# The first layer's feed-forward stage also splits the second mixer's weights, which then come ready split from DRAM

## The chip, the cores and the metric

The kernel runs on one core of a Trainium2 chip. The metric is the device time of one execution in microseconds (us), the median of three runs. All weights and the input lie in DRAM (HBM) when the execution starts, already rearranged on the host.

## The reference

Two blocks follow each other on x, 512 tokens by 1024 channels, in float32. The first has two layers, each a mixer and a feed-forward stage; the second has two layers with other mixers, cross attention and a gated feed-forward stage. The change touches layers 0 and 1 of the first block:

```python
for l in range(2):
    h = rmsnorm(x, norm_mix_g[l])
    proj = h @ w_in[l]                              # 1024 x 4896
    (qa, ka, va, qd, kd, vd, beta_logit, decay_logit, z, gate_logit) = split(proj)
    y_attn = grid_attention(rope(rms(qa)), rope(rms(ka)), va) @ w_o_attn[l]
    qd, kd, vd = silu(conv5(concat(qd, kd, vd)))    # depthwise over tokens
    qd, kd = l2norm(qd), l2norm(kd)
    o = bidir_gated_deltanet(qd, kd, vd, beta, g)   # chunks of 64 tokens, both directions
    y_dn = (rmsnorm(o) * silu(z)) @ w_o_dn[l]
    x = x + (gates[0] * y_attn + gates[1] * y_dn) @ w_out[l]
    h = rmsnorm(x, norm_ffn_g[l])
    u_gate, u_val = split(conv3(h @ w_up[l]))       # 1024 x 5632
    x = x + (silu(u_gate) * u_val) @ w_down[l]      # 2816 x 1024
```

## The kernel before, in words

x is kept transposed, as eight tiles of 128 channels by 512 tokens. Each float32 factor of a large product is split in two parts, a rounded one (hi, type float32r) and the rest (lo), and a product is three matmuls: hi by hi, hi by lo, lo by hi. Activations are split once a stage; weights are split as they are used.

The weights lie in groups of 256 output columns: a group of 1024 input rows is 1 MB, on 128 partitions. `wload` (L464) takes one group. `fetch` (L459, the DMA at L461, on SyncE's queue, SP) brings it into a raw tile `wraw`, of which there are two. Then it is cut into four pieces of 128x512 (four k-chunks of 128 rows by 128 output columns): a copy on ScalarE (ACT, L474) rounds a piece to `whi`, and a subtraction on GpSimd (POOL, the helper `tt`, L383) leaves the rest in `wlo`. There are four buffers of each. `proj` (L480) then issues 12 matmuls for each piece (L487, L490, L491), so that a group is 48 matmuls for two output tiles. Products go to PSUM tiles `psb`, `psf` and `ps`.

The stages come one after the other: m0 (mixer, layer 0), f0 (feed-forward, layer 0), m1, f1, and then the second block. In the profiled execution f0 runs from about 500 to 900 us and m1 from about 900 to 1400.

The feed-forward stage is `ffn`. `up_pair` makes two of 22 middle tiles out of two weight groups: convolution of three taps on ACT and DVE (L588, L589), a gate, a split of the product into `mid`. `down` calls `out_proj` for the products back into x, four groups at a time. The order in the program is five calls of `up_pair`, `down(0)`, four `up_pair`, `down(1)`, two `up_pair`, `down(2)`: 34 groups.

The mixer is `_mix`. Its 19 groups of `win` are, by number: 0 to 3 the query and key tiles of the delta net (`qk_pair`), 4 and 5 its values (`vproj`), 6 and 7 attention's queries, 8 its keys and values, 9 and 10 the output gate z, 11 to 18 the two branch gates (`gate_logits`). `conv_tile` (L697) has a convolution of five taps on DVE; `l2` norms queries and keys; `inside` makes each chunk's inner products and their decays, with tiles `s3`, `gr`, `kt` and `nt` (L843 and after), and stores them to DRAM scratch tiles dnscr (L850, L851), scrK (L836), scrN (L855) and scrT (L863), all on SP; `solve` loads N from scrN and scrT and inverts 64x64 triangles on DVE. `rs_cols` and `rsqrt` make reciprocal roots by integer arithmetic and Newton steps on small 128x16 tiles on DVE (`rc`, `rsq`; L394, L397, L398 and the helper L383). In `_mix`, generators that yield a number are interleaved by a small scheduler that balances those numbers.

The final order of each engine's instructions and of the SP queue is set by the tile framework's scheduler with its own simulated timeline: it may pull an instruction ahead of others as far as buffers allow. On the chip each engine, and each DMA queue, works in its order.

Of the kernel before, what the change touches and what calls it, by code (L numbers as in the profile page):

```python
# [11 lines left out]
F32 = mybir.dt.float32  # L12
# [8 lines left out]
P = 128  # L21
# [23 lines left out]
def _pack_cols(w, kc, cg):  # L45

    w = np.asarray(w)
    L, K, N = w.shape
    g = N // cg
    a = w.reshape(L, kc, P, g, cg).transpose(0, 3, 2, 1, 4)  # L50
    return np.ascontiguousarray(a).reshape(L, g, P, kc * cg)


# [152 lines left out]
def host_arrays(inputs):  # L206
    g = lambda k: np.asarray(inputs[k])
    A = {}
    A["x"] = np.ascontiguousarray(g("x")[0].T).reshape(8, P, S)
    A["mem"] = _pack_cols(np.asarray(g("mem_2")).transpose(0, 2, 1), 8, NMEM)[0, 0]  # L210
    A["vec"] = _vec_layout(inputs)[1]
    A["cst"] = CST_ARR
    A["rope"] = np.ascontiguousarray(_rope_tables())
    A["rett"] = _ret_tables()
    A["hgm"] = _hg_masks()
    A["dsat"] = _dsa_tables()
    A["relb"] = np.concatenate([g("rel_bias_2"), np.ones((1, 8), np.float32)], axis=0)
# [12 lines left out]
    A["wod"] = _pack_cols(by_head(g("w_o_dn").transpose(0, 2, 1)).transpose(0, 2, 1), 4, 128)  # L230
    A["wout"] = _pack_cols(g("w_out"), 8, 256)
    A["wup"] = _pack_cols(g("w_up"), 8, 256)
    for nm, key in (("wdn", "w_down"), ("fdn", "ffn_w_out_2")):
        w = g(key)
        A[nm] = np.concatenate([_pack_cols(w[:, :1024], 8, 256), _pack_cols(w[:, 1024:2048], 8, 256)], axis=1)
        A[nm + "c"] = _pack_cols(w[:, 2048:], 6, 256)
# [3 lines left out]
    A["evin"] = _pack_cols(np.concatenate(ev, axis=2).reshape(1, D, 4096), 8, 256)  # L240
    A["evout"] = _pack_cols(np.concatenate([eo[:, 1 - i, h] for i, h in EV_HEADS], axis=1), 8, 256)

    od = g("od_w_in_2").reshape(1, D, 3, 8, P).transpose(0, 1, 3, 2, 4).reshape(1, D, 3072)
    A["odin"] = _pack_cols(od, 8, 256)
    A["odout"] = _pack_cols(g("od_w_out_2"), 8, 256)
    A["xaq"] = _pack_cols(g("xa_w_q_2"), 8, 256)
    A["xakv"] = _pack_cols(g("xa_w_kv_2"), 8, 256)
    A["xao"] = _pack_cols(g("xa_w_o_2"), 8, 256)
    A["fup"] = _pack_cols(g("ffn_w_in_2"), 8, 256)
    return A  # L250
# [55 lines left out]
class Prog:  # L306
    def __init__(self, ctx, tc, A, out, first):
# [10 lines left out]
        self.dr = pool("dr", 1, space=DRAM)  # L318
        self.ph = None

        self.vect = self.cp.tile([P, NVEC], F32, name="vect")
# [136 lines left out]

    def fetch(self, src, kc, cg):  # L459
        raw = self.wr.tile([P, kc, cg], F32, name="wraw", tag="wraw")  # L460
        self.nc.sync.dma_start(out=raw, in_=src.rearrange("p (k c) -> p k c", k=kc))  # L461
        return raw

    def wload(self, src, kc, cg, rows=False):  # L464


        nc = self.nc
        raw = self.first.pop(0) if self.first else self.fetch(src, kc, cg)
        step, width = (2, cg) if rows else (4, min(P, cg))

        def piece(k, o):
            part = raw[:, k:min(k + step, kc), o:o + width]
            hi, lo = (self.whl.tile(list(part.shape), F32R, name=n, tag=n) for n in ("whi", "wlo"))
            nc.scalar.copy(hi, part)  # L474
            self.tt(lo, part, hi.bitcast(F32), ALU.subtract, "gpsimd")
            return k, hi, lo

        return [[piece(k, o) for k in range(0, kc, step)] for o in range(0, cg, width)]

# [50 lines left out]
    def out_proj(self, wsrc, acts, nxt, k0=0, scale=None, final=True, behind=None):  # L530
        nc = self.nc
        kc = len(acts)
        for g in range(4):
            ws = self.wload(wsrc[g][:, k0 * 256:(k0 + kc) * 256], kc, 256)
# [23 lines left out]
    def ffn(self, l, second, nm, nxt):  # L558
# [3 lines left out]
        with self.phase("ffn") as fp, self.banks(2, 2):  # L562
# [48 lines left out]
            def up_pair(mp):  # L611
                wg = self.wload(wup[mp], 8, 256)
                wv = self.wload(wup[11 + mp], 8, 256)
                for j in range(2):
                    v = (up2 if second else up1)(2 * mp + j, wg[j], wv[j])
                    mid = self.gs("mid", 12, (P, 2, S), F32R)
                    self.split(mid, v)
                    mids[2 * mp + j] = mid

            def down(gi):  # L620
# [12 lines left out]
            for mp in range(9, 11):  # L633
                up_pair(mp)
            down(2)

# [5 lines left out]
    def _mix(self, l, nm, nxt, mp):  # L642
        nc, tc = self.nc, self.tc
        win = self.A["win"][l]
        col = lambda name, n=64: mp.tile([P, n], F32, name=name)
        blk64 = self.c("blk64")
# [55 lines left out]
        def qk_pair(g, first, a):  # L702
            ws = self.wload(win[g], 8, 256)
            for j in range(2):
# [100 lines left out]
        def vproj():  # L805
            for g in range(4, 6):
                ws = self.wload(win[g], 8, 256)
                for j in range(2):
# [80 lines left out]
        def qkv():  # L889


            ws = self.wload(win[8], 8, 256)
            kr, sq = gained(ws[0], f"kg{l}")
# [17 lines left out]
        def queries(g):  # L911


            ws = self.wload(win[6 + g], 8, 256)
            qs = []
# [66 lines left out]
        def zproj():  # L982
            for g in range(9, 11):
                ws = self.wload(win[g], 8, 256)
                for j in range(2):
# [9 lines left out]
        def gate_logits(base, res, make):  # L995
            for g in range(4):
                ws = self.wload(win[base + g], 8, 256)
                for j in range(2):
# [621 lines left out]
    def _cross(self, l, nm, nxt, xp):  # L1620
# [51 lines left out]
        for h in range(4):  # L1672
# [14 lines left out]
            ws = self.wload(wkv[4 + h], 8, 256, rows=True)  # L1687
            vt = [gs("vt", 4, (P, 2, M), F32R) for _ in range(2)]
            pv = [self.psb() for _ in range(2)]
            for t in range(2):  # L1690
                tok = slice(t * P, (t + 1) * P)
                o = pv[t][:, :M]
                for k, hi, lo in ws[0]:
                    for i in range(2):
# [95 lines left out]
```

## Time and profile before

| | |
|---|---|
| median of three runs | 3457.84 us (3456.24 to 3459.11) |
| profiled execution | 3445.89 us |
| its span | 3444.1 us |
| TensorE (PE) busy | 3227.7 us, 94% |
| VectorE (DVE) busy | 2030.8 us, 59% |
| ScalarE (ACT) busy | 1483.2 us, 43% |
| GpSimd (POOL) busy | 1806.1 us, 52% |
| DMA | 342.53 MB, mean 99 GB/s |

The span is the time from the first to the last instruction of the profiled execution. Busy times are of the whole span; the share of one stage can be far from them, so that a stage is read from a cut of the span into stretches. POOL's largest group in the page is the subtraction wlo<-wraw,whi, 1044 instructions and 1369.1 us, and ACT's largest is the cast whi<-wraw, 1044 instructions and 631.5 us.

### The profile page before, as it was taken

How to read it: one execution, taken by the hardware profiler on the slowest of the kernel's cores; microseconds unless marked ns; L12 is line 12 of the kernel's file. 1: busy time of each engine (PE TensorE's matmuls, PEld its weight loads, DVE VectorE, ACT ScalarE, POOL GpSimd, SP SyncE). 2: the span in 40 equal slices, each digit the busy share in tenths (PEclk: the TensorE clock that was granted, in tenths of full speed). 3: DMA queues.
4: the chain of work that ended last, by engine and by line, in shares of the span. 5: the costliest groups of instructions: out<-in, count | busy, mean ns of one | idle time of the engine just before them, and what ended most of it. 6: DMA issues, size and time to landing. Idle time of an engine off the chain costs nothing. (4 is left out here: it accounts for less than half of the span.)

```text
span 3444.1 us, 46891 instructions
## 1 busy us (share of the span) xinstructions
PE 3227.7 (94%) x17342; PEld 2655.6 (77%) x17342; DVE 2030.8 (59%) x3571; ACT 1483.2 (43%) x2766; POOL 1806.1 (52%) x1493
## 2 busy tenths in 40 slices
PE   8888899999987889999999898999999998999999
PEld 6666778888766667788877776878888887888887
DVE  8988555554698866464466676553223786653222
ACT  4526534343553553443353325443334444544332
POOL 4653365444565434654456556565556335555554
PEclk9999999999998999999999998999999999999999
DMA  4532542222354234222232113223223212222222
GB/s 148 160 89 62 119 127 98 98 89 92 121 158 124 73 81 133 100 99 92 98 112 86 62 47 103 85 99 121 94 98 107 78 67 101 88 87 98 98 97 87
DMA packets 135869, 342.53 MB, mean 99 GB/s; under 512 B 43056, under 2 KB 80304, under 8 KB 106969
## 3 DMA queue, kind: packets, MB, share of 16 engines
q1 hardware_dynamic: 134208, 336.04, 30.5%
q10 hardware_dynamic: 1432, 3.49, 0.4%
q8 instruction: 138, 2.26, 0.3%
q14 instruction: 91, 0.74, 0.1%
HBM read 312.15 MB, written 29.97 MB: 99 GB/s over the span
## 5 line engine op out<-in xcount | busy, mean ns | idle before, releaser
L383 POOL TENSOR_TENSOR wlo<-wraw,whi 128x512 fp32r<-128x512 f32 (+2 forms) x1044 | 1369.1, 1316 | 1397.9 <-ACT whi L474 1359.6
L474 ACT CAST whi<-wraw 128x512 fp32r<-128x512 f32 (+2 forms) x1044 | 631.5, 608 | 1129.5 <-PE psb L490 835.2
L487 PE MATMUL psb<-act,whi 128*128 128x512 f32 x1888 | 758.8, 402 | 59.6 <-DVE x L383 19.6
L491 PE MATMUL psb<-act,wlo 128*128 128x512 f32 x1888 | 751.5, 399 | 3.2 <-POOL wlo L383 3.0
L490 PE MATMUL psb<-act,whi 128*128 128x512 f32 x1888 | 752.6, 399 | 0.8 <-DVE act L277 0.6
L487 PEld LDWEIGHTS psb<-act,whi 128*128 128x128 f32 x1888 | 363.5, 193 | 140.0 <-issue 43.4
L491 PEld LDWEIGHTS psb<-act,wlo 128*128 128x128 f32 x1888 | 362.2, 192 | 81.1 <-POOL wlo L383 5.6
L490 PEld LDWEIGHTS psb<-act,whi 128*128 128x128 f32 x1888 | 363.4, 192 | 75.0 <-DVE act L277 2.3
L383 DVE TENSOR_TENSOR x<-psb,x 128x512 f32<-128x512 f32 x168 | 115.2, 689 | 377.0 <-PE psb L491 376.6
L487 PE MATMUL ps<-act,whi 128*128 128x512 f32 (+1 forms) x720 | 280.7, 390 | 3.4 <-ACT rB L303 3.4
L491 PE MATMUL ps<-act,wlo 128*128 128x512 f32 (+1 forms) x720 | 280.2, 389 | 0.0
L490 PE MATMUL ps<-act,whi 128*128 128x512 f32 (+1 forms) x720 | 280.2, 389 | 0.0
L487 PE MATMUL psb<-mid,whi 128*128 128x512 f32 x704 | 276.7, 394 | 1.0 <-DVE x L383 1.0
L491 PE MATMUL psb<-mid,wlo 128*128 128x512 f32 x704 | 276.2, 392 | 0.0
L490 PE MATMUL psb<-mid,whi 128*128 128x512 f32 x704 | 273.6, 389 | 0.0
L487 PEld LDWEIGHTS ps<-act,whi 128*128 128x128 f32 (+1 forms) x720 | 133.9, 186 | 33.7 <-ACT rB L303 4.6
L491 PEld LDWEIGHTS ps<-act,wlo 128*128 128x128 f32 (+1 forms) x720 | 133.9, 186 | 29.4
L490 PEld LDWEIGHTS ps<-act,whi 128*128 128x128 f32 (+1 forms) x720 | 133.9, 186 | 29.1
L491 PEld LDWEIGHTS psb<-mid,wlo 128*128 128x128 f32 x704 | 132.1, 188 | 30.5
L487 PEld LDWEIGHTS psb<-mid,whi 128*128 128x128 f32 x704 | 132.3, 188 | 29.3 <-DVE x L383 1.5
L490 PEld LDWEIGHTS psb<-mid,whi 128*128 128x128 f32 x704 | 132.1, 188 | 29.5
L383 DVE TENSOR_TENSOR cv<-ps,cv 128x512 f32<-128x512 f32 (+1 forms) x60 | 41.5, 692 | 175.9 <-PE ps L491 106.5
(437 smaller groups left out, 5712.3 us busy)
## 6 DMA issues: line engine op xcount, KB each, us to landing
wraw<-in_wup SPq DMA_DIRECT2D x44, 1024.0 KB, 4.8
wraw<-in_fup SPq DMA_DIRECT2D x44, 1024.0 KB, 4.8
wraw<-in_win SPq DMA_DIRECT2D x38, 1024.0 KB, 5.0
wraw<-in_wdn SPq DMA_DIRECT2D x16, 1024.0 KB, 4.8
wraw<-in_evin SPq DMA_DIRECT2D x16, 1024.0 KB, 4.8
wraw<-in_xakv SPq DMA_DIRECT2D x16, 1024.0 KB, 4.9
wraw<-in_fdn SPq DMA_DIRECT2D x16, 1024.0 KB, 4.8
wraw<-in_odin SPq DMA_DIRECT2D x12, 1024.0 KB, 4.9
```

The lines of the kernel that those rows point to most:

```text
L383: getattr(self.nc, eng).tensor_tensor(out, a, b, op)
L474: nc.scalar.copy(hi, part)
L487: mm = nc.tensor.matmul(ps, hi[:, i], acts[k][:, 0, :n], start=k == 0, stop=False)
L490: nc.tensor.matmul(ps, hi[:, i], acts[k][:, 1, :n], start=False, stop=False)
L491: nc.tensor.matmul(ps, lo[:, i], acts[k][:, 0, :n], start=False, stop=k == kc - 1)
```

## The change

Three things are changed.

The host lays weight groups out so that each piece of four k-chunks by 128 columns lies together on a partition (`_pack_tiles`); `fetch` then makes `wraw` of shape (128, columns/128, k-chunks, 128), and `out_proj` passes the k-range that it wants instead of a slice. The splitting of a piece is moved to a helper `parts`, and the cross attention's value groups, which take pieces of two k-chunks by 256 columns, to a helper `wrows`.

`split_ahead` is a generator made in `ffn` of layer 0. For each of the 19 groups of `win` of layer 1 it makes a DRAM tile of two halves; for each half it loads 512 KB into `araw` (three buffers), rounds it on ACT into the first part of a tile `ahl` (two buffers), subtracts on POOL into its second part, and stores both parts, 1 MB, to DRAM. One group is taken after each `up_pair` and after each group of `out_proj`, through `self.side`, 19 calls in all before `down(2)`.

In layer 1, `wgroup` calls `wload_split`: each piece's hi and lo come by a DMA of 256 KB each (128x512) from that DRAM tile directly into `whi` and `wlo`. ACT and POOL do nothing for them.

By the program's counts POOL issues 1460 instructions instead of 1498, ACT 2608 instead of 2646, SP 831 instead of 622; PE and DVE have the same numbers.

The core of the diff:

```diff
+def _pack_tiles(w, kc):
+
+    a = _pack_cols(w, kc, 256)
+    L, g = a.shape[:2]
+    return np.ascontiguousarray(a.reshape(L, g, P, kc, 2, P).transpose(0, 1, 2, 4, 3, 5)).reshape(L, g, P, kc * 256)
...
-    A["win"] = _pack_cols(np.concatenate([kd, qd, vd, qa, ka, va, z, gate], axis=-1), 8, 256)
+    A["win"] = _pack_tiles(np.concatenate([kd, qd, vd, qa, ka, va, z, gate], axis=-1), 8)
...
+    def fetch(self, src, kc, cg, k0=0, n=None):
+
+        n, w = n or kc, min(P, cg)
+        raw = self.wr.tile([P, cg // w, n, w], F32, name="wraw", tag="wraw")
+        self.nc.sync.dma_start(out=raw, in_=src.rearrange("p (j k c) -> p j k c", k=kc, c=w)[:, :, k0:k0 + n])
+        return raw
+
+    def parts(self, part):
+
+        nc = self.nc
+        hi, lo = (self.whl.tile(list(part.shape), F32R, name=n, tag=n) for n in ("whi", "wlo"))
+        nc.scalar.copy(hi, part)
+        self.tt(lo, part, hi.bitcast(F32), ALU.subtract, "gpsimd")
+        return hi, lo
+
+    def split_ahead(self, pool, name, groups):
+
+        nc = self.nc
+        for i, src in enumerate(groups):
+            dst = self.dr.tile([P, 2, 2, 1024], F32, name=f"{name}{i}")
+            self.ahead[name, i] = dst
+            for j in range(2):
+                raw = pool.tile([P, 1024], F32, name="araw", tag="araw", bufs=3)
+                nc.sync.dma_start(out=raw, in_=src[:, j * 1024:j * 1024 + 1024])
+                t = pool.tile([P, 2, 1024], F32R, name="ahl", tag="ahl", bufs=2)
+                nc.scalar.copy(t[:, 0], raw)
+                self.tt(t[:, 1], raw, t[:, 0].bitcast(F32), ALU.subtract, "gpsimd")
+                nc.sync.dma_start(out=dst[:, j], in_=t.bitcast(F32))
+            yield
+
+    def wload_split(self, src):
+
+        def piece(j, k):
+            hi, lo = (self.whl.tile([P, 4, P], F32R, name=n, tag=n) for n in ("whi", "wlo"))
+            for i, t in enumerate((hi, lo)):
+                self.nc.sync.dma_start(out=t.bitcast(F32), in_=src[:, j, i, k * P:(k + 4) * P].rearrange("p (k c) -> p k c", c=P))
+            return k, hi, lo
+
+        return [[piece(j, k) for k in (0, 4)] for j in range(2)]
+
+    def wload(self, src, kc, cg=256, k0=0, n=None):
+
+
+        raw = self.first.pop(0) if self.first else self.fetch(src, kc, cg, k0, n)
+        n = raw.shape[2]
+        return [[(k, *self.parts(raw[:, j, k:min(k + 4, n)])) for k in range(0, n, 4)] for j in range(raw.shape[1])]
...
+            if self.side:
+                self.side()
...
+            later = iter(())
+            if not second and l == 0:
+                later = self.split_ahead(fp, "win", [self.A["win"][1][g] for g in range(19)])
+            self.side = lambda: next(later, None)
...
+            self.side = None
+            for _ in later:
+                pass
             down(2)
...
+        wgroup = lambda g: self.wload_split(self.ahead["win", g]) if l else self.wload(win[g], 8, 256)
...
-            ws = self.wload(win[g], 8, 256)
+            ws = wgroup(g)
```

On POOL, in f0, before: the subtractions of weight pieces stand one after another; what comes between them are the memsets of the next stages' padding. L383 is the helper `tt`.

```order
L383 TENSOR_TENSOR wlo<-wraw,whi 128x512
L683 MEMSET pad_7930 128x2
L684 MEMSET pad_7930 128x2
L683 MEMSET pad_7931 128x2
L684 MEMSET pad_7931 128x2
L383 TENSOR_TENSOR wlo<-wraw,whi 128x512 x117
L383 TENSOR_TENSOR wlo<-wraw,whi 128x256
```

On POOL, in f0, now (the helper is L393, and ahl is the tile that is stored to DRAM): after every one to four pieces of f0's own weights stands a subtraction of twice the width.

```order
L393 TENSOR_TENSOR wlo<-wraw,whi 128x512 x3
L393 TENSOR_TENSOR ahl<-araw,ahl 128x1024
L393 TENSOR_TENSOR wlo<-wraw,whi 128x512
L393 TENSOR_TENSOR ahl<-araw,ahl 128x1024
L393 TENSOR_TENSOR wlo<-wraw,whi 128x512 x4
L393 TENSOR_TENSOR ahl<-araw,ahl 128x1024
L393 TENSOR_TENSOR wlo<-wraw,whi 128x512
L393 TENSOR_TENSOR ahl<-araw,ahl 128x1024
L393 TENSOR_TENSOR wlo<-wraw,whi 128x512 x3
L393 TENSOR_TENSOR ahl<-araw,ahl 128x1024
```

So 38 subtractions of 128x1024 stand in f0's order, all of them within its first 21 weight groups, and the pieces of win of layer 1 no longer stand in m1's.

On SP, in m1 before, where `inside` stores its tiles (L850 and L851 dnscr, L836 scrK, L855 scrN): between the stores stand the fetches of whole weight groups.

```order
L850 DMA dnscr_7895<-s3_8674 64x1024
L850 DMA dnscr_7895<-s3_8674 64x2x512
L461 DMA wraw_9110<-in_win 128x2048
L836 DMA scrK_7908<-kt_8575 128x512
L851 DMA dnscr_7895<-s3_8588 64x512 x2
L851 DMA dnscr_7895<-s3_8674 64x512 x2
L850 DMA dnscr_7895<-s3_8759 64x1024
L850 DMA dnscr_7895<-s3_8759 64x2x512
L855 DMA scrN_7896<-x_8208 128x8x64
L850 DMA dnscr_7895<-s3_8845 64x1024
L850 DMA dnscr_7895<-s3_8845 64x2x512
L461 DMA wraw_9201<-in_win 128x2048
```

On SP, in the same place now (L504 the loads of ready split pieces, win9 the DRAM tile of group 9; L904, L889 and L908 the stores):

```order
L504 DMA whi_9203<-win9_6573 128x512
L504 DMA wlo_9204<-win9_6573 128x512
L504 DMA whi_9207<-win9_6573 128x512
L504 DMA wlo_9208<-win9_6573 128x512
L904 DMA dnscr_8142<-s3_8996 64x512 x2
L904 DMA dnscr_8142<-s3_9080 64x512
L889 DMA scrK_8155<-kt_8983 128x512
L904 DMA dnscr_8142<-s3_9080 64x512
L908 DMA scrN_8143<-x_8457 128x8x64
L504 DMA whi_9211<-win9_6573 128x512
L504 DMA wlo_9212<-win9_6573 128x512
```

Where one fetch of 1 MB stood, eight loads of 256 KB stand, each of which waits until PE is done with a buffer of `whi` or `wlo`.

## Rows read from the trace of the kernel before

**Rows 1.** The page, part 1: busy time of each engine in the whole span.
```profile
PE 3227.7 (94%) x17342; PEld 2655.6 (77%) x17342; DVE 2030.8 (59%) x3571; ACT 1483.2 (43%) x2766; POOL 1806.1 (52%) x1493
```

**Rows 2.** Stretches: per engine busy us and count, granted clock, DMA share, GB/s.
```profile
5.00:15.00 10.00, 5.03 (x11) 3.08 (x11) 6.85 (x7) 7.63 (x16) 7.51 (x6) 1.00 1.05 410
500.00:900.00 400.00, 398.64 (x1751) 327.16 (x1750) 205.35 (x239) 164.61 (x270) 209.67 (x173) 1.00 0.28 100
...
960.00:1240.00 280.00, 228.47 (x1120) 182.98 (x1119) 246.94 (x382) 142.08 (x280) 141.83 (x97) 0.94 0.38 104
```

**Rows 3.** Waits of PE, 960 to 1240: us in total, times, longest.
```profile
PE psb L487 <- DVE x L383: 9.9, 4, 3.8
PE psb L487 <- DVE N L383: 5.8, 1, 5.8
PE ps L798 <- DVE cv L513: 5.7, 1, 5.7
```

**Rows 4.** DVE in order of time: start us, us, instruction.
```profile
1109.90 0.62 DVE L383 TENSOR_TENSOR ntmp<-N 128x456 f32<-128x456 f32 x1
1110.44 1.23 DVE L394 TENSOR_SCALAR rc<-rsq 128x16 int32<-128x16 int32 x1
1111.59 0.62 DVE L383 TENSOR_TENSOR N<-N,ntmp 128x456 f32<-128x456 f32 x1
1112.13 1.23 DVE L383 TENSOR_TENSOR rsq<-rc 128x16 f32<-128x16 f32 x1
...
1114.43 0.16 DVE L397 SCALAR_TENSOR_TENSOR rsq<-rsq 128x16 f32<-128x16 f32 x1
```

**Rows 5.** POOL in order of time, the same stretch.
```profile
1108.21 5.12 POOL L383 TENSOR_TENSOR wlo<-wraw,whi 128x512 fp32r<-128x512 f32 x3
```

**Rows 6.** DVE groups, 960 to 1240: busy us, mean ns | idle before.
```profile
L697 DVE SCALAR_TENSOR_TENSOR cv<-pad,vect,cv 128x512 f32<-128x512 f32 x16 | 16.6, 1041 | 1.0 <-ACT cv L695 0.8
L843 DVE SCALAR_TENSOR_TENSOR s<-kq,eg 128x512 f32<-128x512 f32 x8 | 13.4, 1699 | 0.0
L383 DVE TENSOR_TENSOR x<-x,kkqq 128x512 f32<-128x512 f32 x8 | 12.0, 1523 | 0.0
...
L397 DVE SCALAR_TENSOR_TENSOR rsq<-rsq 128x16 f32<-128x16 f32 x6 | 6.2, 1035 | 0.1
...
L383 DVE TENSOR_TENSOR rsq<-rc 128x16 f32<-128x16 f32 x6 | 5.3, 884 | 0.1
...
L398 DVE SCALAR_TENSOR_TENSOR rc<-rsq,rc 128x16 f32<-128x16 f32 x6 | 4.8, 808 | 0.1
```

**Rows 7.** Durations of one, ns min/median/max, 900 to 1400.
```profile
L697 DVE SCALAR_TENSOR_TENSOR kq<-pad,vect,kq x32: 730/752/1793, 915.0 to 973.1; 128x512 f32<-128x512 f32 x32
...
L397 DVE SCALAR_TENSOR_TENSOR rsq<-rsq x21: 161/191/1276, 908.2 to 1341.8; 128x32 f32<-128x32 f32 x9, 128x16 f32<-128x16 f32 x6, 128x4 f32<-128x4 f32 x3, 128x8 f32<-128x8 f32 x3
```

**Rows 8.** POOL groups, 960 to 1240: busy us, mean ns | idle before.
```profile
L383 POOL TENSOR_TENSOR wlo<-wraw,whi 128x512 fp32r<-128x512 f32 x51 | 75.4, 1486 | 69.4 <-ACT whi L474 69.1
```

**Rows 9.** POOL and ACT groups: wlo at 500 to 900; L1660 whole span.
```profile
L383 POOL TENSOR_TENSOR wlo<-wraw,whi 128x512 fp32r<-128x512 f32 x140 | 187.8, 1341 | 177.9 <-ACT whi L474 175.3 <-PE psb L490 1.4 <-PE psb L491 1.0
...
L383 POOL TENSOR_TENSOR wlo<-wraw,whi 128x256 fp32r<-128x256 f32 x8 | 6.6, 828 | 4.1 <-ACT whi L474 4.1
...
L1660 ACT ACTIVATE msq<-wraw 128x1024 f32<-128x1024 f32 x4 | 4.0, 1044 | 0.0
```

**Rows 10.** DVE groups, 500 to 900, as in rows 6.
```profile
L589 DVE SCALAR_TENSOR_TENSOR cv<-pad,vect,cv 128x512 f32<-128x512 f32 x44 | 53.8, 1225 | 1.1
```

**Rows 11.** DMA issues on SP in order of time: start us, us.
```profile
956.10 10.06 SPq L786 DMA_DIRECT2D x<-scrG  x16
```

**Rows 12.** Waits of the SP queue, 900 to 1400.
```profile
SPq L850 <- DVE s L843: 25.9, 7, 15.8
```

**Rows 13.** DMA issues: count, KB each, median us to landing.
```profile
wraw<-in_win SPq DMA_DIRECT2D x38, 1024.0 KB, 5.0
...
x<-xsp SPq DMA_DIRECT2D x8, 256.0 KB, 2.9
```

More of the change, by code (lines that the diff above doesn't have):

```diff
@@ L230, in host_arrays @@
     A["wod"] = _pack_cols(by_head(g("w_o_dn").transpose(0, 2, 1)).transpose(0, 2, 1), 4, 128)
-    A["wout"] = _pack_cols(g("w_out"), 8, 256)
-    A["wup"] = _pack_cols(g("w_up"), 8, 256)
+    A["wout"] = _pack_tiles(g("w_out"), 8)
+    A["wup"] = _pack_tiles(g("w_up"), 8)
     for nm, key in (("wdn", "w_down"), ("fdn", "ffn_w_out_2")):
         w = g(key)
-        A[nm] = np.concatenate([_pack_cols(w[:, :1024], 8, 256), _pack_cols(w[:, 1024:2048], 8, 256)], axis=1)
-        A[nm + "c"] = _pack_cols(w[:, 2048:], 6, 256)
+        A[nm] = np.concatenate([_pack_tiles(w[:, :1024], 8), _pack_tiles(w[:, 1024:2048], 8)], axis=1)
+        A[nm + "c"] = _pack_tiles(w[:, 2048:], 6)
     ev, eo = g("ev_w_in_2").reshape(1, D, 8, 4, P), g("ev_w_out_2").reshape(1, 2, 4, P, D)
     ev = [ev[:, :, 5]] + [ev[:, :, (slice(0, 4), [4, 6, 7])[i == 0], h] for i, h in EV_HEADS]
-    A["evin"] = _pack_cols(np.concatenate(ev, axis=2).reshape(1, D, 4096), 8, 256)
-    A["evout"] = _pack_cols(np.concatenate([eo[:, 1 - i, h] for i, h in EV_HEADS], axis=1), 8, 256)
+    A["evin"] = _pack_tiles(np.concatenate(ev, axis=2).reshape(1, D, 4096), 8)
+    A["evout"] = _pack_tiles(np.concatenate([eo[:, 1 - i, h] for i, h in EV_HEADS], axis=1), 8)
     od = g("od_w_in_2").reshape(1, D, 3, 8, P).transpose(0, 1, 3, 2, 4).reshape(1, D, 3072)
[L244 to L249, printed above, removed]
+    A["odin"] = _pack_tiles(od, 8)
+    A["odout"] = _pack_tiles(g("od_w_out_2"), 8)
+    A["xaq"] = _pack_tiles(g("xa_w_q_2"), 8)
+    w = g("xa_w_kv_2")
+    A["xakv"] = np.concatenate([_pack_tiles(w[..., :1024], 8), _pack_cols(w[..., 1024:], 8, 256)], axis=1)
+    A["xao"] = _pack_tiles(g("xa_w_o_2"), 8)
+    A["fup"] = _pack_tiles(g("ffn_w_in_2"), 8)
     return A
@@ L319, in __init__ @@
         self.ph = None
+        self.ahead, self.side = {}, None
         self.vect = self.cp.tile([P, NVEC], F32, name="vect")
@@ L456, in spread @@
         return ps
-    def fetch(self, src, kc, cg):
-        raw = self.wr.tile([P, kc, cg], F32, name="wraw", tag="wraw")
-        self.nc.sync.dma_start(out=raw, in_=src.rearrange("p (k c) -> p k c", k=kc))
[L462 to L478, printed above, removed]
+    def fetch(self, src, kc, cg, k0=0, n=None):
[3 more added lines that the diff above has]
+        return raw
@@ L480, in proj, with wrows @@
+    def wrows(self, src, kc):
+        raw = self.wr.tile([P, kc, 256], F32, name="wraw", tag="wraw")
+        self.nc.sync.dma_start(out=raw, in_=src.rearrange("p (k c) -> p k c", k=kc))
+        return [(k, *self.parts(raw[:, k:k + 2])) for k in range(0, kc, 2)]
     def proj(self, ps, w, acts, n=S, behind=None):
@@ L533, in out_proj @@
         for g in range(4):
-            ws = self.wload(wsrc[g][:, k0 * 256:(k0 + kc) * 256], kc, 256)
+            ws = self.wload(wsrc[g], wsrc[g].shape[-1] // 256, k0=k0, n=kc)
             for j in range(2):
@@ L618, in up_pair @@
                     mids[2 * mp + j] = mid
+                self.side()
             def down(gi):
@@ L806, in vproj @@
             for g in range(4, 6):
-                ws = self.wload(win[g], 8, 256)
+                ws = wgroup(g)
                 for j in range(2):
@@ L889, in qkv @@
         def qkv():
-            ws = self.wload(win[8], 8, 256)
+            ws = wgroup(8)
             kr, sq = gained(ws[0], f"kg{l}")
@@ L911, in queries @@
         def queries(g):
-            ws = self.wload(win[6 + g], 8, 256)
+            ws = wgroup(6 + g)
             qs = []
@@ L983, in zproj @@
             for g in range(9, 11):
-                ws = self.wload(win[g], 8, 256)
+                ws = wgroup(g)
                 for j in range(2):
@@ L996, in gate_logits @@
             for g in range(4):
-                ws = self.wload(win[base + g], 8, 256)
+                ws = wgroup(base + g)
                 for j in range(2):
@@ L1686, in _cross @@
                 self.split(kn[-1], x)
-            ws = self.wload(wkv[4 + h], 8, 256, rows=True)
+            ws = self.wrows(wkv[4 + h], 8)
             vt = [gs("vt", 4, (P, 2, M), F32R) for _ in range(2)]
@@ L1692, in _cross @@
                 o = pv[t][:, :M]
-                for k, hi, lo in ws[0]:
+                for k, hi, lo in ws:
                     for i in range(2):
```

## The prediction

> **What bounds the kernel now.** I read the busy shares of the whole span first. TensorE (PE) is busy 94% of 3444.1 us and no other engine over 59% [rows 1]: on average PE is the limit, and work taken off another engine is worth something only where PE stands waiting. So the second view is a cut of the span into stretches. From 500 to 900 us the first feed-forward layer runs (f0), and PE is busy 398.64 of 400 us, with GpSimd (POOL) busy 209.67 and the DMA engines at 28% and 100 GB/s [rows 2]. From 960 to 1240 us the second layer's mixer m1 makes its projections, and there PE is busy only 228.47 of 280 us: 51.5 us are idle. VectorE (DVE) is busy 246.94 of the 280, 88%, and the clock that PE was granted is 0.94 on average, where it is 1.00 in f0 [rows 2]. The third view is what ended PE's waits in that stretch: the largest groups are waits for DVE (tiles x, N and cv), with longest ones of 3.8 to 5.8 us [rows 3]. So m1's projections are set by DVE, not by PE and not by the weights.
>
> Why DVE is so full is seen when its operations are laid beside POOL's. A 128x16 operation on DVE lasts 0.16 us at 1114.43 and 1.23 us at 1110.44 and 1112.13 [rows 4]; in the second case POOL is in the middle of three weight subtractions (wlo) which together take 5.12 us, 1.70 us each [rows 5], against 1.341 us on average in f0 [rows 9]. The two engines hold each other up: a short DVE operation lasts until the POOL operation is over, and POOL then waits its turn. The same DVE line has minimum, median and maximum 161, 191 and 1276 ns, another 730, 752 and 1793 [rows 7].
>
> **The change part by part.** (1) *m1 no longer splits weights.* 76 casts on ACT and 76 subtractions on POOL go from m1; 51 of the subtractions lie in the stretch, 75.4 us, 1486 ns each [rows 8]. What DVE gains: six groups there have means far above their undisturbed duration. With 0.730 us for a 128x512 operation and 0.161 us for a 128x16 one (the minima of rows 7), the excess is 8 x (1.699 - 0.730) = 7.8, 8 x (1.523 - 0.730) = 6.3, 16 x (1.041 - 0.730) = 5.0, 6 x (1.035 - 0.161) = 5.2, 6 x (0.884 - 0.161) = 4.3 and 6 x (0.808 - 0.161) = 3.9, together 32.5 us [rows 6, 7]. Not all of it is beside wlo, as POOL has other work: wlo is 75.4 of POOL's 141.83 us, 53% [rows 2, 8], so 17 us. Since DVE sets this stretch, I count these 17 us in full. PE's clock comes back in part: 0.06 x 280 = 16.8 us of full clock is not granted [rows 2]; the waits shrink from 51.5 by about a third, so I take a third, 5.6 us. Together -23 us. The bounds: nothing, if the waits left are latencies of other chains, and -51.5, if PE never waited there.
>
> (2) *How m1 gets its weights.* A group of 1 MB becomes eight loads of 256 KB, 152 in all, on the in-order SP queue. 16 issues there take 10.06 us, 0.63 us each [rows 11]; a load of 256 KB lands 2.9 us after its issue, one of 1 MB after 5.0 [rows 13]. A load can only be issued when PE gives up one of four buffers, so three pieces are ahead. A matmul takes 398.64/1751 = 0.228 us [rows 2], a piece of 12 takes 2.7 us, three 8.2 us. A piece needs 2 x 0.63 + 2.9 = 4.2 us, so it is hidden while SP is free. SP is not always free: it waits for DVE's tile s before the delta-net stores, 25.9 us in 7 waits, the longest 15.8 [rows 12], and weights now queue behind them where before two raw MB and four split pieces were ahead. A single block of 15.8 us costs up to 15.8 + 4.2 - 8.2 = 11.8 us; several, perhaps 20. And a load that waits for PE holds up what is queued behind it: by the order these are the stores of the delta net's tiles (dnscr, scrK, scrN, scrT), for whose reload the solve on DVE waits (PE's wait for N is its end, [rows 3]). On the other side, a less crowded DVE makes s earlier. I take +2, bounds 0 and +20, nearest to the free case since only one wait can exceed the lead by much.
>
> (3) *The split in f0.* 38 pieces of 128x1024, each an ACT copy, a POOL subtraction, a load of 512 KB and a store of 1 MB. By the order they lie in f0's first 21 weight groups, 1.8 to a group. No POOL subtraction of this width is in the trace. From 128x512 (1341 ns) and 128x256 (828 ns) [rows 9] one extrapolates 1.341 + 2 x 0.513 = 2.37 us; twice the 128x512 is 2.68. I take 2.4, as the difference of two widths leaves a fixed part once: 38 x 2.4 = 91 us. Only a page gives such a price directly: the Trainium skill, "GPSIMD Engine Reference", section "Performance versus the Vector engine", has 4497 ns for twice this width, which halved and taken 38 times makes about 85 us, an estimate; with it the sum is the same. ACT takes 1.044 us for 128x1024 [rows 9], 40 us in all beside its 164.61 in 400 [rows 2]: covered. POOL: a group is 48 matmuls, 10.9 us; 4 x 1.341 + 1.8 x 2.4 = 9.7 us, 89% of it. That fits, but with little to spare, and DVE's two convolution operations per tile (44, 1225 ns each [rows 10], against 0.730 undisturbed) will be longer still and push POOL back. If every wlo took the 1.70 us of rows 5, and each piece 0.36 more, a group would need 4 x 1.70 + 1.8 x 2.76 = 11.8 us, 0.9 over, 19 us in 21 groups; part of this the lead of three to four split pieces takes up. DMA: a group moves 1.05 MB of its own and 1.8 x (0.52 + 1.05) more, 3.9 MB in 10.9 us, 358 GB/s, where the busiest stretch of this trace, with loads alone, moved 410 [rows 2]. On SP a store of ahl waits for POOL, and the next fetch of a weight group is queued behind it; its lead is two raw groups, some 20 us. I take +6 for all three, bounds 0 and +45 (the rival below).
>
> (4) *The repacked weights.* Each fetch moves the same bytes and each split piece is the same size. What covers a slower fetch is that two are in flight against 10.9 us a group, with 5.0 to land [rows 13]; without cover, each would cost the 5 us. I take 0.
>
> **Sum:** -23 + 2 + 6 = -15 us on the profiled execution (3445.89 us, of which the span is 3444.1). That execution lies 12 us under the median of three, 3457.84, which is 0.35%; I carry the difference over: 3457.84 - 15 = 3443.
>
> **The rivals.** *A, slower: f0 becomes bound by its extra traffic or by POOL.* PE in f0 has no slack (398.64 of 400 us), so every us by which a group is late is a us of the kernel. The price: if stores with loads reach not 410 but 300 GB/s, a group takes 3.9/300 = 13.0 us, 2.1 over, 44 us in 21 groups; -23 + 44 = +21, about 3479. It decides at 358 GB/s: above that there is nothing to pay. Against it: 410 was reached, and the extra pieces end after 21 of f0's groups, so that a late piece can be made up behind them. For it: no stretch of the trace shows loads and stores together near that rate, and POOL at 89% is just as near its edge. The pair of DVE and POOL bears on it: the trace shows 1.23 us instead of 0.16 where they overlap [rows 4], and f0 gets 91 us more of such overlap. The Trainium skill, "Perfetto Trace Analysis", section "Optimizing Scalar/DVE Operations", says that GpSimd and VectorE share an SBUF read port, so that moving work between them might not help; by that rule the work is only moved to another stretch, and rows 4 and 5 agree with the sharing. But it is a gain if f0's DVE has room, which at 205.35 of 400 us [rows 2] it has.
>
> *B, no change: the waits of 960 to 1240 are latencies, not throughput.* DVE's chains are sequential, with PE, ACT and DRAM round trips between, such as the wait for N [rows 3]. Then the 17 us shrink to about 8, f0 takes 6 to 8 back, and the time is 3458. Against it: DVE at 88%.
>
> *C, weights late in m1.* The feed at its bound of 20 us: -23 + 20 + 6 = +3, 3461, no change either. For it: the 15.8 us wait [rows 12]; against it: it is only one.
>
> **How the numbers follow.** The forecast gets 0.57, A 0.25, B 0.10, C 0.08. What can be told from no change is 0.2%, 6.9 us: so faster (under 3451) 0.57, same 0.18, slower (over 3465) 0.25. The range goes from 3413 (two thirds of the 51.5 and the clock regained, -45) to 3478, nearly all of A. The forecast's own range is 3413 to 3451, nearest to its middle the 3443.
>
> **What would show it.** Right: from 960 to 1240, or what these projections now take, PE's idle time falls from 51.5 to about 30 us and the clock rises to about 0.96; the six groups of rows 6 fall to near 0.73 and 0.16 us; POOL's wlo is gone there; f0 keeps PE busy within 6 us of now, with POOL about 300 of 400 us busy. Step 2 is wrong if PE's waits in m1 end on loads of whi or wlo for over 5 us in all. Step 3 is wrong if PE waits in f0 for wlo or whi for over 10 us. Wrong altogether: f0 longer by over 20 us, or idle time in m1 unchanged.

## The result, and the profile after

The changed kernel takes 3475.06 us (median; 3471.18 to 3478.55), the kernel before, timed beside it, 3457.04: a ratio of 1.0052, 95% interval 1.0035 to 1.0070. It is slower, by 18 us; forecast was 15 faster. The profiled execution of after has a span of 3472.7 us.

The starts of three instructions cut the span into stretches: the first convolution of f0 (tile cv: 553.2 us before, 562.1 after), m1's copy of its gate logits (raw) and the last copy of the solve (N). From cv to raw PE has the same work in both (1698 and 1699 matmuls); from raw to N it has not (881 and 840), which Step 1 below takes up. The tile view of DVE gives first and last start; before:

```profile
L743 DVE COPY raw<-ps x2: 282/282/282, 47.6 to 933.2; 128x128 f32<-128x128 f32 x2
L1037 DVE COPY N<-N x1: 1025/1025/1025, 1159.8 to 1159.8; 64x1024 f32<-64x1024 f32 x1
```

and after:

```profile
L796 DVE COPY raw<-ps x2: 291/292/292, 50.0 to 979.1; 128x128 f32<-128x128 f32 x2
L1090 DVE COPY N<-N x1: 1075/1075/1075, 1177.0 to 1177.0; 64x1024 f32<-64x1024 f32 x1
```

From cv to raw (f0 and m1's start) 380.0 us became 417.0, 37.0 more. From raw to N (m1's projections) 226.6 became 197.9, 28.7 less. Ahead of cv, at f0's norm, 5.9 us were lost: from the first cast of m0's mixed product (478.3 and 481.3) 74.9 us became 80.8. So f0, with m1's start, costs some 43 us and m1 gives 29 back, 14 of the 18 us. The two spans are 28.6 us apart, but 11.1 of that lie behind m1, in work that the change doesn't touch (from f1's first convolution to the end 2006.6 and 2017.7 us; 2008.4 in layout and 2011.7 in f0_only, two runs below whose m1 is as before), and the profiled execution of before is 11 us under its median.

In the windows of after, f0 and m1's projections (columns as in [rows 2]):

```profile
545.00:900.00 355.00, 328.13 (x1388) 262.96 (x1387) 223.63 (x194) 154.78 (x236) 261.60 (x153) 0.97 0.70 252
980.00:1260.00 280.00, 248.96 (x1252) 205.28 (x1251) 228.08 (x425) 124.63 (x247) 66.82 (x46) 0.95 0.59 166
```

PE, which was idle 1.4 of 400 us in f0 [rows 2], is idle 26.9 of 355, and the clock is granted at 0.97 on average, for 1.00. Of the 37.0 us from cv to raw, 22.6 are idle time; the other 14.4 are busy time, as 1699 matmuls took 394.07 us at a mean clock of 0.98 where 1698 took 379.68 at 1.00. POOL is busy 261.60 us, 74%; DMA moves 252 GB/s. PE's waits, 500 to 960 us:

```profile
PE ps L533 <- POOL wlo L393: 12.7, 9, 2.9
PE ps L529 <- ACT whi L480: 6.4, 5, 3.5
PE ps L465 <- DVE nrc L408: 5.7, 1, 5.7
```

The first two are for split weights, the third is for the norm; a further 2.1 us are a wait for a ready split weight at m1's start. POOL's two groups, 545 to 900 us:

```profile
L393 POOL TENSOR_TENSOR wlo<-wraw,whi 128x512 fp32r<-128x512 f32 x115 | 164.7, 1445 | 73.6 <-ACT whi L480 73.3
L393 POOL TENSOR_TENSOR ahl<-araw,ahl 128x1024 fp32r<-128x1024 f32 x38 | 99.6, 2622 | 20.6 <-ACT ahl L494 20.6
```

In the norm, DVE's timeline has what [rows 4] showed, at twice the length: a 128x4 operation beside a wide subtraction takes 2.32 us (0.16 for the same operation before) and is over when POOL's is, at 550.9; another takes 0.17 where nothing runs beside it.

```profile
548.61 2.32 DVE L393 TENSOR_TENSOR nsum<-nsum 128x4 f32<-128x4 f32 x1
...
553.46 0.17 DVE L404 TENSOR_SCALAR nrc<-rsq 128x4 int32<-128x4 int32 x1
```

The convolution, in DVE's tile view of after (ns min/median/max):

```profile
L633 DVE SCALAR_TENSOR_TENSOR cv<-pad,vect,cv x44: 737/1668/2898, 562.8 to 912.9; 128x512 f32<-128x512 f32 x44
```

Before:

```profile
L589 DVE SCALAR_TENSOR_TENSOR cv<-pad,vect,cv x44: 740/753/1836, 554.0 to 870.8; 128x512 f32<-128x512 f32 x44
```

VectorE's operations that read one operand from PSUM, where PE leaves its products, did not grow: pad<-psb,rB has 675/684/694 ns in after and 683/685/694 before. In m1, the groups of [rows 6] are shorter (980 to 1260 us):

```profile
L750 DVE SCALAR_TENSOR_TENSOR cv<-pad,vect,cv 128x512 f32<-128x512 f32 x16 | 15.5, 972 | 2.5 <-ACT cv L748 2.4
L896 DVE SCALAR_TENSOR_TENSOR s<-kq,eg 128x512 f32<-128x512 f32 x8 | 10.2, 1290 | 0.0
L393 DVE TENSOR_TENSOR x<-x,kkqq 128x512 f32<-128x512 f32 x8 | 7.5, 952 | 0.0
L393 DVE TENSOR_TENSOR rsq<-rc 128x16 f32<-128x16 f32 x6 | 4.0, 675 | 0.1
L407 DVE SCALAR_TENSOR_TENSOR rsq<-rsq 128x16 f32<-128x16 f32 x6 | 3.8, 640 | 0.1
L408 DVE SCALAR_TENSOR_TENSOR rc<-rsq,rc 128x16 f32<-128x16 f32 x6 | 2.1, 352 | 0.1
```

### The profile page after: what moved, and what is told of

Read it like the earlier page. It is cut to its first block, busy times and chain, and to the rows that moved or that the text cites. A ratio compares the mean times of both kernels' runs of the same rounds, so it can differ in the third digit from the quotient of the medians.

```text
span 3472.7 us, 47146 instructions
## 1 busy us (share of the span) xinstructions
PE 3240.8 (93%) x17342; PEld 2663.1 (77%) x17342; DVE 2043.1 (59%) x3571; ACT 1473.7 (42%) x2728; POOL 1804.9 (52%) x1455
## 5 line engine op out<-in xcount | busy, mean ns | idle before, releaser
L393 POOL TENSOR_TENSOR wlo<-wraw,whi 128x512 fp32r<-128x512 f32 (+2 forms) x968 | 1270.6, 1318 | 1189.1 <-ACT whi L480 1139.0
L480 ACT CAST whi<-wraw 128x512 fp32r<-128x512 f32 (+2 forms) x968 | 583.4, 607 | 1065.1 <-PE psb L532 788.3
L393 DVE TENSOR_TENSOR x<-psb,x 128x512 f32<-128x512 f32 x168 | 115.1, 688 | 374.5 <-PE psb L533 374.1
L533 PE MATMUL ps<-act,wlo 128*128 128x512 f32 (+1 forms) x720 | 284.1, 395 | 12.7 <-POOL wlo L393 12.7
L529 PE MATMUL ps<-act,whi 128*128 128x512 f32 (+1 forms) x720 | 285.1, 396 | 9.7 <-ACT whi L480 6.4
L532 PE MATMUL ps<-act,whi 128*128 128x512 f32 (+1 forms) x720 | 283.4, 394 | 0.0
L393 DVE TENSOR_TENSOR cv<-ps,cv 128x512 f32<-128x512 f32 (+1 forms) x60 | 41.5, 692 | 177.2 <-PE ps L533 106.8
```

What stands on the lines that cost most here:

```text
L393: getattr(self.nc, eng).tensor_tensor(out, a, b, op)
L529: mm = nc.tensor.matmul(ps, hi[:, i], acts[k][:, 0, :n], start=k == 0, stop=False)
L532: nc.tensor.matmul(ps, hi[:, i], acts[k][:, 1, :n], start=False, stop=False)
L533: nc.tensor.matmul(ps, lo[:, i], acts[k][:, 0, :n], start=False, stop=k == kc - 1)
```

## The experiments

Ratios are to the kernel before, timed beside each run, with 95% intervals. "f0" is cv to raw, "m1" raw to N, in us of the profiled execution (before 380.0 and 226.6, the change 417.0 and 197.9). The f0 column holds the same work of PE in every run (1693 to 1701 matmuls). The m1 column doesn't: 881 matmuls where m1 splits its own weights, 824 to 864 where it doesn't, so that a few us in it can be work put off behind N.

| run | ratio | f0 | m1 |
|---|---|---|---|
| layout | 1.0007 (0.9996 to 1.0017) | 380.0 | 226.7 |
| f0_only | 1.0128 (1.0114 to 1.0142) | 413.1 | 226.4 |
| m1_only | 0.9959 (0.9946 to 0.9972) | 385.0 | 199.4 |
| no_sub | 0.9961 (0.9946 to 0.9977) | 383.6 | 198.2 |
| no_store | 1.0067 (1.0053 to 1.0081) | 420.6 | 197.2 |
| even | 1.0044 (1.0032 to 1.0056) | 416.3 | 198.4 |
| even_dve | 0.9962 (0.9948 to 0.9975) | 389.1 | 198.2 |
| even_small | 1.0004 (0.9993 to 1.0014) | 403.0 | 198.0 |
| dve_change | 0.9955 (0.9939 to 0.9972) | 382.7 | 192.7 |
| even_256 | 1.0175 (1.0160 to 1.0190) | 464.9 | 199.6 |
| dve_small | 0.9947 (0.9934 to 0.9960) | 387.8 | 198.7 |
| dve_own | 0.9936 (0.9923 to 0.9949) | 384.7 | 192.9 |
| in_up | 1.0010 (1.0000 to 1.0021) | 399.4 | 195.1 |
| in_down | 0.9983 (0.9973 to 0.9992) | 389.0 | 195.9 |
| buf_256 | 0.9943 (0.9929 to 0.9956) | 388.5 | 198.4 |
| dve_best | 0.9930 (0.9914 to 0.9945) | 378.7 | 196.3 |
| buf_1024 | 1.0035 (1.0023 to 1.0047) | 415.5 | 198.7 |
| buf_small | 0.9992 (0.9982 to 1.0003) | 407.4 | 199.1 |

### The parts alone

layout leaves out both uses of the split weights:

```diff
-            if not second and l == 0:
+            if False:
...
-        wgroup = lambda g: self.wload_split(self.ahead["win", g]) if l else self.wload(win[g], 8, 256)
+        wgroup = lambda g: self.wload(win[g], 8, 256)
```

> Only the repacked weights and the helpers of the change; no group is split ahead, and layer 1's mixer splits its own weights as before. All theories: the bytes and the pieces are the same, so 3457 us, within 5 of the kernel before. If the strides of the weight tiles mattered it would be off by more, and part of the 18 us would be theirs.

No change: the repacked weights cost nothing. f0_only has the second of these edits alone:

> The splitting in the first feed-forward layer is done and stored in full, but layer 1's mixer does not use it: it fetches and splits its own weights as before. All theories of the first feed-forward layer: its loss alone, about 43 us by the landmarks of the two traces (the mixer's first raw tile came 45.9 us later, of which 2.4 were there in the first mixer), so about 3500. If the loss came from the ready split weights being late at the start of the mixer, it would be less.

1.0128 of 3452.36 is 44 us, as expected. In its trace f0 is 33.1 us longer and the norm 5.7; the change's other 3.9 us from cv to raw are m1's start. m1_only:

```diff
-                later = self.split_ahead(fp, "win", [self.A["win"][1][g] for g in range(19)])
+                later = self.split_ahead(fp, "win", [self.A["win"][1][0]])
...
-        wgroup = lambda g: self.wload_split(self.ahead["win", g]) if l else self.wload(win[g], 8, 256)
+        wgroup = lambda g: self.wload_split(self.ahead["win", 0]) if l else self.wload(win[g], 8, 256)
```

> Only one group is split ahead; layer 1's mixer loads that same group 19 times over, by the same 152 loads as in the change, and splits nothing. The results of that mixer are therefore those of other weights. Theory that the gain is VectorE's and GpSimd's relief there: 28 us (45.9 us late at its start, 17.2 at the end of the triangular solve), so about 3429. If part of the 28 us was only catching up with work that had been delayed, it is less, 3440 to 3450.

A gain of 14 us, less than the 28 expected. m1's projections do win 27 us (199.4; over the whole of m1, from raw to f1's first convolution, 26), but 5 are given back at m1's start (385.0), and 3.6 ahead of f0: the one group's two pieces stand beside the norm (74.9 became 78.5). no_sub stores ScalarE's copy twice:

```diff
-                self.tt(t[:, 1], raw, t[:, 0].bitcast(F32), ALU.subtract, "gpsimd")
-                nc.sync.dma_start(out=dst[:, j], in_=t.bitcast(F32))
+                nc.sync.dma_start(out=dst[:, j], in_=t.bitcast(F32).unsqueeze(1).broadcast_to((P, 2, 1024)))
```

> The change without GpSimd's 38 subtractions: ScalarE's copy is stored into both halves, with the same loads, the same bytes stored and the same queue. The results of layer 1's mixer therefore lack the low parts. Theory 1 (GpSimd and VectorE in each other's way in the first feed-forward layer): the loss there goes, at most 8 us stay, so 3430 to 3440. Theory 2 (the DMA engines, at 82 to 87% there): the loss stays, 3470 to 3475. Theory 3 (weight fetches queued on SP behind stores that wait for GpSimd, 206 us of such waits): the stores now wait only for ScalarE, the loss goes as with theory 1; another run has to tell 1 from 3.

The loss is gone, with all of the DMA traffic in place. In its window f0 has 263 GB/s, more than the change's 252, and PE idles 1.8 us:

```profile
545.00:900.00 355.00, 353.21 (x1555) 290.70 (x1554) 182.88 (x219) 177.28 (x272) 178.94 (x137) 1.00 0.72 263
```

### Where the subtractions cost

For these runs the pieces are tied behind f0's own weight pieces, on ScalarE and GpSimd, by a list of positions that counts those (where VectorE subtracts, its place is left to the scheduler); of the diff:

```diff
-                nc.scalar.copy(t[:, 0], raw)
-                self.tt(t[:, 1], raw, t[:, 0].bitcast(F32), ALU.subtract, "gpsimd")
+                self.issue_behind(nc.scalar.copy(t[:, 0], raw), c)
+                self.issue_behind(nc.gpsimd.tensor_tensor(t[:, 1], raw, t[:, 0].bitcast(F32), ALU.subtract), s)
```

no_store has the change's own positions, and stores and uses group 0 alone:

> GpSimd's 38 subtractions, ScalarE's copies and the loads stand at the places of the change, but only the first group is stored and layer 1's mixer loads that one 19 times (results of other weights). So no fetch on SP stands behind a store that waits for GpSimd. Theory 1 (GpSimd and VectorE in each other's way): the loss of the first feed-forward layer stays, 35 to 43 us over the run without subtractions (0.996 of before), so 1.006 to 1.009 of before. Theory 3 (fetches late behind stores on SP): the loss goes, 0.996 to 0.998.

The loss stays: it is not the stores. This run can't clear the loads of araw, which still wait on SP until POOL gives up a buffer, with f0's fetches queued behind them. But in the change ACT's casts waited for a fetched weight only once, 3.6 us (ACT's waits, 545 to 960 us), so late fetches look to be no more of the loss than that.

even has positions 10, 13, 16 and so on:

> The change with its 38 pieces tied to places: one behind every third of the layer's own weight pieces, from the 10th to the 121st of 136, on ScalarE and on GpSimd; the same work in the same layer. Theory 1: a group then has 4 subtractions and 1.3 pieces, 4 x 1.34 + 1.3 x 2.6 = 8.8 of 10.9 us (the change: 1.8 pieces, 10.1), and the norm at the layer's start has no piece beside it; the loss falls from 43 to 5 to 15 us and the kernel is at 0.996 to 1.000 of before. If the loss goes with the number of pieces wherever they stand (so much per piece), it stays at 1.005.

The norm's 5.9 us are back (74.9), but f0 is as long as in the change (416.3): spreading the pieces did nothing, and theory 1 as I had it, with rows that fill up, was wrong. even_dve is even with the subtraction on nc.vector:

> As the run with the pieces spread evenly, but the subtraction of a piece is VectorE's. Theory 1a (GpSimd's own time is what is short: its row is full and VectorE has room): the loss goes almost wholly, 0.994 to 0.997 of before. Theory 1b (what is short is the time that the two share): VectorE's 38 operations over two SBUF inputs, some 1.3 us each alone, hold GpSimd up as long as they last, and the gain over the run before is small, within 0.002 of it.

Theory 1a's number, though its reason, GpSimd's full row, falls with buf_256 below. VectorE's 38 operations cost little: f0 is 4 us longer than in m1_only (385.0), whose m1 starts in the same way. even_small is even in 76 pieces of 512 columns:

> As the run with the pieces spread evenly, but in 76 pieces of 512 columns. Theory: VectorE waits for one operation of GpSimd at a time, and these are half as long (1.34 us for 2.6); GpSimd's sum is the same, 76 x 1.34 = 102 us for 99.6. If the length of one matters, 3 to 6 us better than with 38 pieces; if only the sum, the same within 3 us; the 152 DMA issues instead of 76 cost nothing while SP waits.

14 us better, with more work on POOL. So the length of one operation matters, and more than forecast.

dve_change is the change with one word other:

```diff
-                self.tt(t[:, 1], raw, t[:, 0].bitcast(F32), ALU.subtract, "gpsimd")
+                self.tt(t[:, 1], raw, t[:, 0].bitcast(F32), ALU.subtract, "vector")
```

> The change with one word other: the subtraction of a piece is VectorE's, not GpSimd's; where the pieces stand is left to the scheduler, as in the change. Theory: it is GpSimd's wide operation that costs the first feed-forward layer, not the crowding in its first 21 groups. Then 0.995 to 0.998 of before, as with VectorE and spread pieces (0.996). If the crowding counts as well (two pieces beside the norm at the layer's start, ScalarE's copies), 0.999 to 1.002.

0.9955 where the change has 1.0052. Its DVE group, 545 to 900 us:

```profile
L393 DVE TENSOR_TENSOR ahl<-araw,ahl 128x1024 fp32r<-128x1024 f32 x38 | 55.0, 1448 | 12.8 <-ACT ahl L494 12.8
```

### Length against sum

even_256 cuts even's pieces to 256 columns:

> The evenly spread pieces on GpSimd once more, in 152 pieces of 256 columns. The length of one operation falls to 0.83 us alone, the sum rises to 152 x 0.83 = 126 us and more (38 pieces: 97.5 us, 76 pieces: 116). Theory that VectorE's waits behind one long operation cost the time: better than with 76 pieces, 0.997 to 0.999 of before. Theory that GpSimd's sum costs it: worse than with 76, 1.002 to 1.006. With the two against each other: about 1.000, as with 76.

A miss of every expectation, and no answer: another wait had taken over. ACT's waits, 540 to 1000 us:

```profile
ACT ahl L498 <- DMA win<-ahl: 173.9, 106, 6.1
```

Two buffers of 256 columns are too few: ACT stood before its next copy until a store had landed, with its weight casts queued behind. buf_256 has eight such buffers, in the bytes of the change's two, and twelve for araw:

```diff
-                raw = pool.tile([P, 256], F32, name="araw", tag="araw", bufs=3)
+                raw = pool.tile([P, 256], F32, name="araw", tag="araw", bufs=12)
...
-                t = pool.tile([P, 2, 256], F32R, name="ahl", tag="ahl", bufs=2)
+                t = pool.tile([P, 2, 256], F32R, name="ahl", tag="ahl", bufs=8)
```

> 152 evenly spread pieces of 256 columns on GpSimd, with eight buffers for the split pieces instead of two and twelve for the raw ones (the same bytes as in the change), since in the run with two buffers ScalarE waited 173.9 us for them. Theory that the length of GpSimd's operation sets the loss: 0.996 to 0.999 of before, better than with 76 pieces (1.000). Theory that GpSimd's sum sets it (126 us and more for 97.5): 1.003 to 1.008.

The loss is all but gone, on GpSimd itself. Its window of f0, and its group of pieces in the POOL view:

```profile
545.00:900.00 355.00, 350.98 (x1532) 286.27 (x1531) 207.86 (x216) 185.55 (x384) 328.96 (x287) 1.00 0.81 260
```

```profile
L499 POOL TENSOR_TENSOR ahl<-araw,ahl 128x256 fp32r<-128x256 f32 x152 | 144.9, 963 | 0.0
```

POOL is busy 328.96 of 355 us, 93%, and PE idles 4.0 us. f0 is 388.5 us, of which 4 to 5 over 380.0 are m1's start. A full row on GpSimd costs little here; a long operation does. buf_1024 is even with three buffers, buf_small is even_small with four, and six for araw:

> 38 evenly spread pieces of 1024 columns on GpSimd, with three buffers for the split pieces instead of two (more don't fit). Theory that the length of one GpSimd operation sets the loss: 1.004 of before, as with two buffers. Theory that the narrow pieces won by their deeper buffers, not by their length: 0.996 to 1.000.

> 76 evenly spread pieces of 512 columns on GpSimd, with four buffers for the split pieces and six for the raw ones (the same bytes as in the change; with two buffers ScalarE waited 46.2 us for them). Theory of length: between the wide pieces (1.0044) and those of 256 columns with enough buffers (0.9943), 0.996 to 0.999 of before, and better than with two buffers (1.0004) by what those 46 us were worth. Theory of the sum of GpSimd's work: GpSimd does less here than with 256 columns, so 0.994 or less.

For the wider pieces buffers are not it: 1.0035 against 1.0044, and 0.9992 against 1.0004. By length the ratios are 1.0035 (1024 columns, 97.6 us of pieces on POOL), 0.9992 (512, 116.8 us) and 0.9943 (256, 144.9 us): the loss falls while the sum rises. The medians of the convolution's two lines go the same way: 1772 and 1664 ns at 1024 columns, 1368 and 1663 at 512, 1014 and 1112 at 256, 873 and 753 before.

A rival is POOL's own order: a weight piece stands behind a long subtraction, and PE waits for it. PE's waits for wlo are 12.7 us in the change, but only 2.4 in even (545 to 960 us), whose f0 is as long. So this can be a part of the change's loss, and is little of even's.

in_up and in_down tie 20 pieces of 1024 columns, of ten groups, behind every second weight piece (the positions and the mixer's `wgroup`, not shown here, follow suit):

```diff
+            if not 4 <= i < 14:
+                continue
```

> Ten of the 19 groups (4 to 13) are split ahead, on GpSimd as in the change, 20 pieces, one behind every second weight piece of up projections, where VectorE has the convolutions; the mixer splits the other nine itself. Theory 1 (the two engines hold each other up): half of the loss of the run with 38 spread pieces (36 us between the layer's first convolution and the mixer's raw tile), 15 to 20 us there. Theory of the sum (GpSimd's own row is too full): the same as in the run with the pieces in the down projections.

> The same ten groups and 20 pieces on GpSimd, one behind every second weight piece, but in the down projections, where VectorE only adds PSUM to x. Theory 1: VectorE has next to nothing there that GpSimd could hold up, and GpSimd nothing that holds it, so the loss is 0 to 6 us and the kernel 10 us or more under the run with the pieces in the up projections. Theory of the sum: the places are as dense (2 x 1.34 + 2.6 us in 5.4 us of PE), so the two are alike within 4 us.

At one density, f0 is 10.4 us shorter with the pieces where VectorE has no convolution. The convolution's median (L636 there) is 1660 ns in in_up and 753 in in_down, as before. in_down's other 9 us over 380.0 are more than the 0 to 6 expected. In its trace ACT waits 12.4 us for stores of ahl (545 to 900 us), in in_up not at all; no run took that away, so their cause is open.

### Versions that beat both

> VectorE's subtractions, spread evenly, in 76 pieces of 512 columns instead of 38 of 1024. GpSimd's weight pieces wait for one VectorE operation at a time, 0.73 us alone instead of some 1.3. Of the 15 us that this could at most give back nothing is seen as PE's wait in the run with 38 pieces (7.6 us from 480 to 960 us in all): within 0.002 of it, 0.994 to 0.998 of before.

Alike with even_dve within the intervals. dve_own keeps groups 0 and 2, the first of m1, out of the split:

```diff
+            if i in (0, 2):
+                continue
...
-        wgroup = lambda g: self.wload_split(self.ahead["win", g]) if l else self.wload(win[g], 8, 256)
+        wgroup = lambda g: self.wload_split(self.ahead["win", g]) if l and g not in (0, 2) else self.wload(win[g], 8, 256)
```

> VectorE's subtractions, spread evenly, but groups 0 and 2, the first that layer 1's mixer uses, are not split ahead: the mixer fetches and splits them as before, so that its first weights don't wait for buffers that PE gives up late. The start of the mixer lost 4 to 5 us in all runs with ready split weights (from the first convolution of the feed-forward layer to the mixer's raw tile 385.0 us with one group split ahead, 380.0 before). If those were late loads: 0.9950 of before, 4 us under the run with all 19. If they are the new order of work: no difference.

> The change with the subtraction on VectorE, places left to the scheduler, and without groups 0 and 2, which the mixer splits itself. The two gains found apart are 0.9955 and, for the two groups, 0.9936 against 0.9962 with spread pieces. If they add: 0.993; if the scheduler's places had already won the second one (its mixer took 192.7 us to the solve's end, as did that of the run without the two groups, 198 in the others): 0.9955.

f0 is 4.4 us (dve_own against even_dve) and 4.0 us (dve_best against dve_change) shorter to the raw tile, and PE's waits for a ready split weight up to there, 2.3 us in even_dve and 1.8 in dve_change, are gone: m1's first loads were late. From cv to f1's first convolution dve_own keeps its gain (860.0 us for 864.9), but dve_best loses it again (861.6 for 858.6). The ratios point the same way, but their intervals overlap or touch, so whether leaving out the two groups pays is not settled. dve_best, 0.9930 (0.9914 to 0.9945), 3432.71 us, is the lowest ratio of all, 23 us under the kernel before; the intervals of dve_own, dve_small, dve_change and buf_256 overlap its own.

## Why the prediction was wrong, point by point

**Step 1, m1's relief: right.** Forecast -23 us, measured -28.7 from raw to N. Between these two starts lies unequal work, 881 matmuls before and 840 now; but from raw to f1's first convolution, with 3045 and 3046, 504.3 us became 475.9, so the gain holds, at 28.4. Of it 21.6 us are idle time of PE (forecast 17) and 6.8 busy time (forecast 5.6, as clock). The six groups of [rows 6] summed to 58.3 us and now to 43.1, 15.2 less for the 17 forecast. Their means did not fall to near 0.73 and 0.16 us, though: they are 0.95 to 1.29 and 0.35 to 0.68, with POOL still busy 66.82 of 280 us. PE's idle time in the two windows fell from 51.5 to 31.0 us of 280 (forecast 30), the clock rose from 0.94 to 0.95.

**Step 2, the feed: near in size, wrong by its own sign.** +2 forecast, 4 to 5 measured, and at m1's start. From 980 to 1260 us PE waited 6.5 us for ready split weights, where over 5 was to show the step wrong. The waits for s on SP that I had feared fell from 25.9 to 2.5 us; ahead of the longest of PE's waits, 4.8 us at 1104.7, SP had stood 5.4 us before a reload of N until scrT was stored.

**Step 3, the split in f0: this step failed.** It was given 6 us, "bounds 0 and +45", and was worth 39 in f0_only's trace and 44 by its ratio. The size of a subtraction was nearly right (2622 ns measured, 2.4 us taken), and POOL was as full as forecast (74% of f0's window for "about 300 of 400"). By the prediction's own sign, over 10 us of PE's waits for wlo or whi, it is wrong: they are 19.1. Wrong was the reasoning that work fits where a row has room. What f0 pays goes not by POOL's sum but by the time for which one of its operations holds up one of VectorE's, which in after lasts up to 2.9 us instead of 0.74. The profile had the sign: [rows 4] showed DVE operations that lasted until POOL's beside them was over, 1.23 us, and with POOL's width doubled that became 2.32. I priced it by [rows 5] as 0.36 us on POOL and not as delay on VectorE's chain in f0, which is six operations to a middle tile (four of convolution, the gate, the split), with ACT's steps between. ACT waits for that chain, ahead of mid and behind the convolutions, and its weight casts stand in its order. ACT's waits, 545 to 900 us, before:

```profile
ACT cv L591 <- DVE cv L589: 37.4, 19, 2.2
ACT mid L496 <- DVE cv L383: 29.0, 20, 2.9
```

and after:

```profile
ACT mid L538 <- DVE cv L393: 51.9, 17, 6.2
ACT cv L635 <- DVE cv L633: 47.0, 17, 7.1
```

Together they are 66.4 us before and 98.9 after, and 70.3 and 74.4 in dve_change and buf_256, where the loss is gone. That this is how the delay comes to PE is read from these waits; no run cut that chain by itself.

**Rival A** had the right size (+21, 3479) by luck: the DMA traffic that was to decide it is harmless (PE idle 1.8 and 4.0 of 355 us in no_sub and buf_256). Its second half, GpSimd beside VectorE, is what happened, but the price was worked out for the first. The Trainium skill, "Perfetto Trace Analysis", section "Optimizing Scalar/DVE Operations", holds that moving work between GpSimd and VectorE may not help, as they share a read port; the sharing agrees with the 2.32 us above, but the move did help here (dve_change, 1.0052 to 0.9955). The same section of the Trainium skill says that breaking up instructions of ScalarE and VectorE may let work finish sooner where those are not full but make others wait; here the same held for GpSimd's (1.0035, 0.9992, 0.9943).

**The price that a page gave.** The Trainium skill, "GPSIMD Engine Reference", section "Performance versus the Vector engine", led to an estimate of 85 us for the 38 subtractions; measured are 99.6.

**Step 4** was right (layout). Rivals B and C did not come about: m1's idle time fell by 20.5 us, and PE's waits for ready split weights in it were 6.5, not the 20 of rival C.

## What to carry to other kernels

A GpSimd operation that is put beside a VectorE chain is priced by its length, not by its share of a row with room: in this kernel a VectorE operation with no operand in PSUM could be held up for the whole of the GpSimd operation beside it (it lasted up to 2.9 us beside one of 2.6, for 0.74 alone). Make such pieces narrow, with buffers for as many bytes as before, or give them to VectorE, where the same subtraction took 1448 ns instead of 2622. And when work is made ahead, try leaving out what the consumer needs first: it took some 4 us off m1's start (dve_own, dve_best), though the whole gain is not settled.

## What the runs showed of the hardware that I had not expected

GpSimd at 93% of a window beside VectorE's convolutions, in operations of 1.46 and 0.96 us, left f0 8.5 us longer, of which 4 to 5 are m1's start; at 74%, in operations of 1.4 and 2.6 us, 37 us longer. VectorE does the 128x1024 subtraction in 1448 ns beside GpSimd's work. And DMA at 0.72 to 0.81 of its engines' time and 260 GB/s, loads and stores mixed, left PE idle only 1.8 to 4.0 of 355 us in f0.
